# The first microseconds of a two-layer hybrid encoder put into one written order

## The chip, the cores and the metric

The kernel runs on one core of a Trainium2 chip. The metric is device time in microseconds of one execution. TensorE (PE) multiplies, VectorE (DVE) and ScalarE (ACT) do the elementwise work, GpSimd (POOL) fills constants and issues some DMAs, SyncE (SP) issues nearly all loads.

## The reference, cut to what matters

One sequence of 256 tokens with 1024 features goes through two layers. In each layer the tokens are normalised, four token mixers (A to D) take slices of one combined projection of the normalised tokens, the four results are gated and summed, and a feed-forward part follows. The edit touches the first normalisation and the first product behind it:

```
xf = x.astype(F32)
y = xf * lax.rsqrt(jnp.mean(xf * xf, axis=-1, keepdims=True) + EPS)
return (y * g.astype(F32)).astype(x.dtype)     # rmsnorm
...
h @ w_in          # slices 3 and 16 of it are the values of mixers A and D
```

## The kernel before, in words

All weights lie in units of 128 x 2048 numbers and are streamed from memory, each as two halves of 512 KB. Each f32 product is made of three fp32r matmuls (`mm3`): a half `raw` is cast on ACT to `hi`, and DVE subtracts to get the rest, `lo`; activations are held in the same way as `ahi` and `ali`. The three products are hi by hi, hi by rest and rest by hi. Four buffers hold `raw`, six `hi`, five `lo`.

The norm (class `Norm`) works on two tiles of 128 tokens, tt = 0 and 1. The squares of a token tile are summed in two halves: for the first half of tile 0 on ACT (`Square`), for its second on DVE (line 202), for tile 1 both on ACT. A square root on ACT, a reciprocal and two `SCALAR_TENSOR_TENSOR` on DVE (line 221) then scale the tile to `xni`; its gain `ng` comes from two matmuls with one row of ones. PE turns `xni` round, 128 x 128 at a time, against the matrix `ident`, into `nti` (line 234), which ACT and DVE split into `ahi` and `ali` (lines 235, 236).

The first product (`tok_units`) is units 3 and 16 together: for each token tile eight steps k, each three matmuls of 128 x 512 into `av`. Steps k = 0 to 3 use unit 3's two halves, k = 4 to 7 unit 16's. Tile 0 is done whole, then tile 1. After it come unit 5 (`bx`) and unit 6 (`bg`) of mixer B, units 0, 1, 2 and 4 (`aq`, `af`, `af`, `ag`) of mixer A, then unit 7 onwards (`c`) of mixer C; between them stand small products for filters, called `f` in the trace: line 369 and 372 make a hidden layer `hd`, a second sine chain on DVE called `sykb` ends in `h2s` (ACT), from which four more `f` products are made, and `bz` (gates of mixer B, with weights `bw`) whose results ACT turns by a sigmoid into `br` and `bi`. Sine, sigmoid, tanh and square root on ACT need tables that are loaded (`ACT_TABLE_LOAD`) where the kind changes.

The order of instructions on an engine is made when the program is built: a scheduler places instructions by priority on an estimated timeline. `tc.high_priority` raises a priority, and `behind(...)` keeps an instruction from standing ahead of a given one. `unit` issues a unit's loads on SP and its casts; all loads stand behind `x_in`, the load of the second token tile. `prepare`, `level_masks` and `filters` make constants on DVE and ACT; in layer 0 they stand behind the last weight load issued.

Of the kernel before, what the change touches and what calls it, by code (L numbers as in the profile page):

```python
# [41 lines left out]
NRAW, NHI, NLO = 4, 6, 5  # L42
@with_exitstack
def trunk(ctx: ExitStack, tc: tile.TileContext, A: dict, out: bass.AP, dbg=None):
    nc = tc.nc
    V, SC, G, PE = nc.vector, nc.scalar, nc.gpsimd, nc.tensor

    cp = ctx.enter_context(tc.tile_pool(name="cp", bufs=1))
    wp = ctx.enter_context(tc.tile_pool(name="wp", bufs=4))
# [38 lines left out]
    x = cp.tile([P, 2, D], F32, tag="x", name="x")  # L88
    nc.sync.dma_start(g0[:1], A["norm1_g"][0:1])
    nc.sync.dma_start(x[:, 0], A["x"][0:P])  # L90
    ident = const("ident", (P,))
    x_in = nc.sync.dma_start(x[:, 1], A["x"][P:S])
    with tc.issue_after(x_in.ins):
        par = const("par", (L, NPC), "params")

# [2 lines left out]
        return par[:, l, c : c + 1]  # L98


    last_load = [None]

    def behind(*ins):

        st = ExitStack()
        for i in ins:
            st.enter_context(tc.issue_after(i.ins))
        return st

    def unit(l, u, after=(), then=None, at=None):  # L110


        parts = []
        with tc.high_priority(offset=AHEAD):
            for hf in range(2):
                raw = wp.tile([P, 1024], F32, tag="raw", bufs=NRAW, name=f"raw{l}_{u}_{hf}")
                if at:
                    hi, lo = (get(f"{n}{l}_{u}_{hf}", F32R).rearrange("p a b -> p (a b)")
                              for n, get in zip(("hi", "lo"), at))
                else:  # L120
                    hi = wp.tile([P, 1024], F32R, tag="hi", bufs=NHI, name=f"hi{l}_{u}_{hf}")
                    lo = wp.tile([P, 1024], F32R, tag="lo", bufs=NLO, name=f"lo{l}_{u}_{hf}")
                with tc.issue_after(x_in.ins):
                    last_load[0] = nc.sync.dma_start(raw, A["wall"][l, u, :, hf * 1024 : hf * 1024 + 1024])
                with behind(*(then if hf and then else after)):
                    SC.copy(hi, raw)  # L126
                    V.tensor_tensor(lo, raw, hi.bitcast(F32), ALU.subtract)  # L127
                parts.append((hi, lo))
        return parts

    def root_table(last):

# [25 lines left out]
                        k + ft == 0, k + ft == 8)  # L158
        return ps

    def tok_units(ws, act, nms, at):

        rows = [t for w in ws for part in w for t in zip(*(p.rearrange("p (k c) -> k p c", k=2) for p in part))]
        out = []
        with ExitStack() as order:
            for tt in range(2):
                ps = big(nms[tt])
                out.append(ps)  # L170
                c = slice(tt * P, tt * P + P)
                for k, w in enumerate(rows):
                    if (tt, k) in at:
                        order.enter_context(behind(at[tt, k](out)))
                    mm = mm3(ps.rearrange("p a b -> p (a b)"),
                             [a[k // 2][:, k % 2, c] if type(a) is list else a[:, k, c] for a in act], w, k == 0, k == 7)
                order.enter_context(behind(mm))
        return out


    class Norm:


        def __init__(self, nm, gain, l=0):
            self.ss = wk.tile([P, 2, 3], F32, tag="ss", bufs=2, name=f"ss{nm}")
            self.rs = wk.tile([P, 2], F32, tag="rs", bufs=2, name=f"rs{nm}")
            if nm == "i":
                self.g = [mix(f"ng{c}").rearrange("p a b -> p (a b)") for c in range(2)]
                for c in range(2):
                    PE.matmul(self.g[c], ones[:1], g0[:1, c * 512 : c * 512 + 512], start=True, stop=True)  # L190
            else:
                g = w4(f"ng{nm}").rearrange("p a b -> p (a b)")
                src = A[gain]
                nc.gpsimd.dma_start(g, bass.AP(src.tensor, src.offset + l * D, [[0, P], [1, D]]))
                self.g = [g[:, c : c + 512] for c in (0, 512)]
            self.xn = [w4(f"xn{nm}{tt}").rearrange("p a b -> p (a b)") for tt in range(2)]
            self.nm, self.hi = nm, None

        def add(self, tt, i, c):

            if (self.nm, tt, i) == ("i", 0, 1):
                V.tensor_tensor_reduce(self.xn[tt][:, c], x[:, tt, c], x[:, tt, c], 1.0, 0.0, ALU.mult, ALU.add,
                                       self.ss[:, tt, 1:2])
            else:
                SC.activation(self.xn[tt][:, c], x[:, tt, c], AF.Square, accum_out=self.ss[:, tt, i : i + 1])
            if not i:
# [628 lines left out]

    SC.activation(epsb2, epsb, AF.Sqrt)
    nm = Norm("i", "norm1_g")
    for tt in range(2):
        for hf in range(2):
            nm.add(tt, hf, slice(hf * 512, hf * 512 + 512))  # L840
        if tt:
            nm.scale(1)
        else:
            nm.half(0)
            turned = nm.scaled, nm.last
    h = nm.out()

    def late(nm):

        return {(0, 6 + dd): lambda _, dd=dd: nm.turn(1, dd) for dd in range(2)}  # L850

    for l in range(L):
        pv = tok_units([unit(l, 3), unit(l, 16, *turned)], h, [f"av0{l}", f"av1{l}"], late(nm))
# [318 lines left out]
```

## Time and profile before

| | |
|---|---|
| median of 3 runs | 1001.65 us (1000.2 to 1003.1) |
| the profiled execution's own time | 999.49 us |
| its span in the trace | 997.6 us |
| PE busy | 976.9 us of the span |
| DVE, ACT busy | 655.4 us, 546.2 us |

The profiled execution is 1.9 us longer than its span, for what lies around the first and the last instruction. It is 2.2 us below the median of the unprofiled runs. Busy time of PE counts matmuls whose ends are modelled; at full clock two neighbouring 128x256 matmuls start 0.12 us apart, and two of 128x512 start 0.23 us apart.

### The profile page before, as it was taken

What the parts mean: (1) busy time and instruction counts of PE and PEld (TensorE: products, weight loads), DVE (VectorE), ACT (ScalarE), POOL (GpSimd) and SP (SyncE); (2) the same over time, 40 slices, a digit from 0 to 9 for tenths busy, and PEclk for the clock granted to TensorE, in tenths of its full rate; (3) what the DMA queues carried; (4) which work ended last, traced back from release to release, by engine and by line L of the source; (5) the groups of instructions that cost most, each with busy time, mean ns of one, the idle gap of its engine ahead of it and who ended that gap; (6) DMA issues with size and microseconds to landing.
All of it is one profiled execution on the core that took longest, in us unless ns stands there. A gap on an engine that the chain in (4) does not pass through costs nothing.

```text
span 997.6 us, 18829 instructions
## 1 busy us (share of the span) xinstructions
PE 976.9 (98%) x7770; PEld 913.2 (92%) x7770; DVE 655.4 (66%) x900; ACT 546.2 (55%) x815; POOL 48.1 (5%) x85
## 2 busy tenths in 40 slices
PE   7999999999999999999999999999999999999997
PEld 5889999999998999999989999999999889999996
DVE  6859894777766764455567679767667575555554
ACT  6696746545745544444457875554454464444442
POOL 0127200000000010000000000000000000000000
PEclk9999999999999999999999999999999999999999
DMA  8648455355555555555546445453465556555551
GB/s 286 202 133 217 135 170 171 116 170 159 183 174 164 187 169 190 188 186 180 186 148 210 162 158 160 158 177 106 163 228 173 170 161 211 187 182 189 187 172 43
DMA packets 51484, 172.41 MB, mean 173 GB/s; under 512 B 8716, under 2 KB 9413, under 8 KB 51398
## 3 DMA queue, kind: packets, MB, share of 16 engines
q1 hardware_dynamic: 47158, 163.41, 50.3%
q0 software_dynamic: 4240, 7.79, 3.1%
q8 instruction: 61, 1.00, 0.4%
q14 instruction: 25, 0.20, 0.1%
HBM read 170.08 MB, written 2.63 MB: 173 GB/s over the span
## 4 chain that ended last, share of the span: by engine, by line
PE 87%; DVE 5%; DMA 4%; ACT 2%; issue 1%; SPq 0%; DVEq 0%; ACTq 0%
PE f L142 9%; PE f L144 9%; PE f L143 8%; PE g L142 6%; PE g L144 6%; PE g L143 6%; PE acc L143 4%; PE acc L142 4%; PE acc L144 4%; DMA raw<-in_wall_dram 3%; DVE lo L127 2%; PE wo L143 1%; PE wo L144 1%; PE wo L142 1%; PE br L142 1%; PE br L143 1%
## 5 line engine op out<-in xcount | busy, mean ns | idle before, releaser
L127 DVE TENSOR_TENSOR lo<-raw,hi 128x1024 fp32r<-128x1024 f32 x304 | 370.2, 1222 | 223.0 <-PE f L143 109.5
L126 ACT CAST hi<-raw 128x1024 fp32r<-128x1024 f32 x304 | 317.5, 1051 | 294.3 <-PE f L144 99.8
L142 PE MATMUL f<-ahm,hi 128*128 128x256 f32 x640 | 181.1, 283 | 0.0
L144 PE MATMUL f<-alm,hi 128*128 128x256 f32 x640 | 181.1, 283 | 0.0
L143 PE MATMUL f<-ahm,lo 128*128 128x256 f32 x640 | 180.2, 282 | 0.0
L143 PEld LDWEIGHTS f<-ahm,lo 128*128 128x128 f32 x640 | 120.9, 189 | 1.0
L142 PEld LDWEIGHTS f<-ahm,hi 128*128 128x128 f32 x640 | 120.7, 189 | 0.9
L144 PEld LDWEIGHTS f<-alm,hi 128*128 128x128 f32 x640 | 120.4, 188 | 0.0
L142 PE MATMUL g<-ahi,hi 128*128 128x256 f32 x256 | 73.3, 286 | 2.1 <-ACT dvt L734 2.1
L144 PE MATMUL g<-alf,hi 128*128 128x256 f32 x256 | 72.8, 284 | 0.0
L142 PE MATMUL g<-ahf,hi 128*128 128x256 f32 x256 | 72.6, 283 | 0.2 <-ACT dvt L734 0.2
L143 PE MATMUL g<-ahf,lo 128*128 128x256 f32 x256 | 72.4, 283 | 0.0
L143 PE MATMUL g<-ahi,lo 128*128 128x256 f32 x256 | 72.3, 283 | 0.0
L144 PE MATMUL g<-ali,hi 128*128 128x256 f32 x256 | 72.3, 282 | 0.0
L143 PE MATMUL acc<-hi,fal 128*128 128x512 f32 x176 | 69.5, 395 | 0.0
L144 PE MATMUL acc<-lo,fah 128*128 128x512 f32 x176 | 69.3, 395 | 0.0
L142 PE MATMUL acc<-hi,fah 128*128 128x512 f32 x176 | 69.1, 395 | 0.0
L142 PEld LDWEIGHTS g<-ahi,hi 128*128 128x128 f32 x256 | 48.2, 188 | 3.3 <-ACT dvt L734 2.3
L142 PEld LDWEIGHTS g<-ahf,hi 128*128 128x128 f32 x256 | 48.2, 188 | 0.6 <-ACT dvt L734 0.4
L144 PEld LDWEIGHTS g<-alf,hi 128*128 128x128 f32 x256 | 48.2, 188 | 0.5 <-issue 0.3
L143 PEld LDWEIGHTS g<-ahi,lo 128*128 128x128 f32 x256 | 48.2, 188 | 0.2 <-issue 0.2
L143 PEld LDWEIGHTS g<-ahf,lo 128*128 128x128 f32 x256 | 48.2, 188 | 0.2 <-issue 0.2
(493 smaller groups left out, 2209.6 us busy)
## 6 DMA issues: line engine op xcount, KB each, us to landing
raw<-in_wall_dram SPq DMA_DIRECT2D x304, 512.0 KB, 4.6
bt<-bias POOLq DMA_DIRECT2D x8, 384.0 KB, 3.8
x<-in_x_dram SPq DMA_DIRECT2D x2, 512.0 KB, 6.1
bias<-tab POOLq DMA_DIRECT2D x16, 64.0 KB, 5.9
ngm<-in_norm_g_dram POOLq DMA_DIRECT2D x2, 512.0 KB, 4.3
out_dram<-x SPq DMA_DIRECT2D x4, 256.0 KB, 2.0
bias<-tab POOLq DMA_DIRECT2D x32, 16.0 KB, 4.3
ngf<-in_norm_g_dram POOLq DMA_DIRECT2D x1, 512.0 KB, 4.1
```

Of the source, the lines that this page charges most:

```text
L126: SC.copy(hi, raw)
L127: V.tensor_tensor(lo, raw, hi.bitcast(F32), ALU.subtract)
L142: PE.matmul(o, a[0], b[0], start=first, stop=False)
L143: PE.matmul(o, a[1], b[0], start=False, stop=False)
L144: return PE.matmul(o, a[0], b[1], start=False, stop=last)
```

## The change

The loads on SP are put in a new order: tokens 0, both halves of unit 3, tokens 1, both halves of unit 16. `ident` is no longer loaded (64 KB); POOL makes it with a memset and an `affine_select`. Eight 128 x 128 matmuls of ones by ones are put ahead of the gain's matmuls. The norm, the casts and the splits of the first two units (new function `first_unit`) are each placed behind the one written ahead of them. The product's steps go by turns: k = 0 to 5 for token tile 0, k = 0 to 5 for tile 1, then k = 6, 7 for tile 0 and for tile 1; the turning of tile 1 stands ahead of step 4 of tile 0 and step 0 of tile 1. The constants of `prepare` and what follows them are placed behind the last split of unit 16 also.

```
+    G.memset(ident, 0.0)
+    G.affine_select(out=ident, in_=ident, compare_op=ALU.not_equal, fill=1.0, base=0, pattern=[[-1, P]],
+                    channel_multiplier=1)
...
-    ident = const("ident", (P,))
-    x_in = nc.sync.dma_start(x[:, 1], A["x"][P:S])
+    raws = {}
+    for u, hf in ((3, 0), (3, 1), (16, 0), (16, 1)):
...
+        x_in = nc.sync.dma_start(raws[0, u, hf][0], A["wall"][0, u, :, hf * 1024 : hf * 1024 + 1024])
+        if (u, hf) == (3, 1):
+            nc.sync.dma_start(x[:, 1], A["x"][P:S])
...
+    def first_unit(u, hf):
+        raw, hi, lo = raws[0, u, hf]
+        return SC.copy(hi, raw), V.tensor_tensor(lo, raw, hi.bitcast(F32), ALU.subtract)
...
+                for _ in range(8):
+                    PE.matmul(self.g[0][:, 0:P], ones, ones, start=True, stop=True)
...
+        for hf in range(2):
+            then(*nm.add(0, hf, halves[hf]))
+        nm.scale(0)
+        then(*nm.scaled)
+        then(*first_unit(3, 0))
+        for dd in range(2):
+            nm.turn(0, dd)
+            then(*nm.last)
+        then(*nm.add(1, 0, halves[0]))
+        then(*first_unit(3, 1))
+        then(*nm.add(1, 1, halves[1]))
+        nm.scale(1)
+        then(*nm.scaled)
+        then(*first_unit(16, 0))
...
+            pv = tok_units(first, h, [f"av0{l}", f"av1{l}"], {(0, 4): lambda _: turn(0), (1, 0): lambda _: turn(1)},
+                           ((0, range(6)), (1, range(6)), (0, range(6, 8)), (1, range(6, 8))))
...
-            with behind(last_load[0]):
+            with behind(last_load[0], *begun):
```

What this does to the order, at three places. The first is DVE at the very start, from the statistics of token tile 0 on (`ssi` statistics, `xni_120` and `xni_121` the scaled tiles, `lo_3_0` the first half's rest). Before:

```order
L202 ISA xni_93,ssi<-x 128x512
L202 ISA ssi 128x1
L208 TENSOR_SCALAR ssi<-ssi 128x1
L213 RECIPROCAL rsi<-rsi 128x1
L221 SCALAR_TENSOR_TENSOR xni_93<-x,rsi,ng_89 128x512
L221 SCALAR_TENSOR_TENSOR xni_93<-x,rsi,ng_90 128x512
L208 TENSOR_SCALAR ssi<-ssi 128x1
L213 RECIPROCAL rsi<-rsi 128x1
L221 SCALAR_TENSOR_TENSOR xni_94<-x,rsi,ng_89 128x512
L221 SCALAR_TENSOR_TENSOR xni_94<-x,rsi,ng_90 128x512
L127 TENSOR_TENSOR lo_3_0_127<-raw_3_0_125,hi_3_0_126 128x1024
L236 TENSOR_TENSOR ali<-nti_104,ahi 128x4x128
```

With the change:

```order
L228 TENSOR_SCALAR ssi<-ssi 128x1
L222 ISA xni_120,ssi<-x 128x512
L222 ISA ssi 128x1
L234 RECIPROCAL rsi<-rsi 128x1
L242 SCALAR_TENSOR_TENSOR xni_120<-x,rsi,ng_108 128x512
L242 SCALAR_TENSOR_TENSOR xni_120<-x,rsi,ng_109 128x512
L144 TENSOR_TENSOR lo_3_0_88<-raw_3_0_86,hi_3_0_87 128x1024
L257 TENSOR_TENSOR ali<-nti_133,ahi 128x4x128
L257 TENSOR_TENSOR ali<-nti_140,ahi 128x4x128
L228 TENSOR_SCALAR ssi<-ssi 128x1
L144 TENSOR_TENSOR lo_3_1_92<-raw_3_1_90,hi_3_1_91 128x1024
L234 RECIPROCAL rsi<-rsi 128x1
```

The small `TENSOR_SCALAR` on `ssi` now stands ahead of the reduce, the first half's rest ahead of the first `ali`, and the scaling of tile 1 behind two rests; by the diff the rest of unit 16's first half comes right behind that scaling.

The second place is ACT between the last query product `aq` and the first gate of mixer B (`br`). Before:

```order
L137 CAST bwh_510<-bw_506 128x512
L454 ACT_TABLE_LOAD
L454 ACTIVATE bt_500<-bt_500 128x512
L346 ACT_TABLE_LOAD
L346 ACTIVATE sykb_308<-sykb_308 128x256
L137 CAST h2s_316<-sykb_308 128x256
L126 CAST hi_4_1_849<-raw_4_1_848 128x1024
L137 CAST bwh_518<-bw_514 128x512
L515 COPY kqe_633<-aq_649 128x512
L516 COPY kqo_634<-aq_649 128x512
```

With the change, from the sine's table load on (the sigmoids of the first `af`, `sf_773` and `sk_774`, stand just ahead):

```order
L367 ACT_TABLE_LOAD
L367 ACTIVATE sykb_319<-sykb_319 128x256
L549 ACTIVATE kqe_644<-sk_774,omlb 128x256 x2
L136 CAST hi_8_0_1004<-raw_8_0_1003 128x1024
L152 CAST h2s_327<-sykb_319 128x256
L136 CAST hi_8_1_1010<-raw_8_1_1009 128x1024
L544 ACT_TABLE_LOAD
L544 ACTIVATE sf_844<-af_794 128x512
L545 ACTIVATE sk_845<-af_794 128x512
L548 ACTIVATE sf_844<-sf_844,lb,omlb 128x256 x2
L549 ACTIVATE kqo_645<-sk_845,omlb 128x256 x2
L496 ACTIVATE br_537<-bz_539,par 128x256
```

The sine of `sykb` and `h2s` stood ahead of the copies of `aq`; now they stand behind the sigmoids of the first `af`, with a table load on either side, and the first `br` stands behind the second `af` as well.

The third place is PE where the first `h2s` products stand. Before, the first of them behind 23 matmuls of the first `af` unit (`af_712`):

```order
L144 MATMUL af_712<-ali,hi_1_0_701 128x256
L142 MATMUL af_712<-ahi,hi_1_0_701 128x256
L143 MATMUL af_712<-ahi,lo_1_0_702 128x256
L142 MATMUL f_000_323<-h2s_316,w3s_291 128x256
L143 MATMUL f_000_323<-h2s_316,w3s_291 128x256
L142 MATMUL f_010_324<-h2s_316,w3s_291 128x256
L143 MATMUL f_010_324<-h2s_316,w3s_291 128x256
```

With the change, behind both `af` units and 22 matmuls of `ag`:

```order
L158 MATMUL ag_865<-ahi,lo_4_0_855 128x256
L159 MATMUL ag_865<-ali,hi_4_0_854 128x256
L157 MATMUL ag_865<-ahi,hi_4_0_854 128x256
L157 MATMUL f_000_334<-h2s_327,w3s_302 128x256
L158 MATMUL f_000_334<-h2s_327,w3s_302 128x256
L157 MATMUL f_010_335<-h2s_327,w3s_302 128x256
L158 MATMUL f_010_335<-h2s_327,w3s_302 128x256
```

They stand 95 matmuls of 128x256 further back; the first `bz` moves with them and stands right behind the eighth.

## Rows read from the trace of the kernel before

**Rows 1.** The profile page, part 1: busy time, share of the span and instructions of each engine.

```profile
PE 976.9 (98%) x7770; PEld 913.2 (92%) x7770; DVE 655.4 (66%) x900; ACT 546.2 (55%) x815; POOL 48.1 (5%) x85
```

**Rows 2.** The waits of PE over the whole run: who waited, for which engine's tile and line; us in total, times, longest.

```profile
PE f L142 <- ACT h2s L137: 3.3, 2, 2.1
PE nti L234 <- DVE xni L221: 2.7, 2, 1.4
PE ng L190 <- DMA g<-in_norm_g_dram: 2.5, 1, 2.5
PE g L142 <- ACT dvt L734: 2.3, 2, 2.1
```

**Rows 3.** Busy time by stretch of the span: the stretch and its length, then busy us of PE, PEld (weight loads), DVE, ACT and POOL with instructions in brackets, granted clock, DMA share, GB/s.

```profile
0.00:18.00 18.00, 12.87 (x35) 8.37 (x36) 10.77 (x22) 12.31 (x23) 0.44 (x6) 1.00 0.87 286
...
50.00:75.00 25.00, 23.63 (x192) 21.32 (x193) 14.97 (x25) 23.85 (x55) 5.42 (x9) 1.00 0.48 133
...
104.00:152.00 48.00, 45.92 (x556) 44.09 (x555) 46.75 (x72) 27.70 (x42) 2.16 (x4) 1.00 0.49 153
```

**Rows 4.** SP's DMA issues at the start, in order of time: start, us, queue, line, what.

```profile
2.49 2.20 SPq L124 DMA_DIRECT2D raw<-in_wall_dram  x4
...
8.13 0.33 SPq L865 DMA_DIRECT2D idft<-in_dft_dram  x1
9.60 0.33 SPq L296 DMA_DIRECT2D maskf<-in_masks_dram  x1
...
13.53 0.31 SPq L359 DMA_DIRECT2D zd<-in_zT_dram  x1
```

**Rows 5.** The timeline of the first 14 us, all engines: start, us, engine, line, operation, out<-in, count [idle time before <- what ended it].

```profile
2.47 3.75 PE L190 MATMUL ng<-g,ones 1*128 1x512 f32 x4 [2.47 <-DMA g<-in_norm_g_dram]
...
5.24 0.69 DVE L202 CUSTOM_DVE_ANT_0 xni<-x 128x512 f32<-128x512 f32 x1 [4.36 <-DMA x<-in_x_dram]
...
6.80 1.41 DVE L221 SCALAR_TENSOR_TENSOR xni<-x,rsi,ng 128x512 f32<-128x512 f32 x2
...
7.60 1.97 PE L234 MATMUL nti<-ident,xni 128*128 128x128 f32 x8 [1.39 <-DVE xni L221]
...
9.71 1.03 ACT L126 CAST hi<-raw 128x1024 fp32r<-128x1024 f32 x1
...
11.36 1.22 DVE L127 TENSOR_TENSOR lo<-raw,hi 128x1024 fp32r<-128x1024 f32 x1
...
11.61 0.78 PE L142 MATMUL av<-hi,ahi 128*128 128x512 f32 x1
...
12.49 1.28 DVE L236 TENSOR_TENSOR ali<-nti,ahi 128x512 fp32r<-128x512 f32 x2
...
13.23 0.79 PE L143 MATMUL av<-hi,ali 128*128 128x512 f32 x1
```

**Rows 6.** The timeline of PE, 14 to 27 us, two pairs of neighbours and the first matmul of the next unit (columns as above).

```profile
14.25 0.63 PE L142 MATMUL av<-hi,ahi 128*128 128x512 f32 x1
14.68 0.63 PE L143 MATMUL av<-hi,ali 128*128 128x512 f32 x1
...
26.29 0.39 PE L144 MATMUL av<-lo,ahi 128*128 128x512 f32 x1
26.52 0.28 PE L142 MATMUL bx<-ahi,hi 128*128 128x256 f32 x1
```

**Rows 7.** The timeline of PE, 30 to 64 us: the rows that had to wait, and the first `bz`.

```profile
34.89 0.70 PE L372 MATMUL f<-hd,hw 64*128 64x256 f32 x2 [0.78 <-ACT hd L346]
...
46.51 0.36 PE L142 MATMUL af<-ahi,hi 128*128 128x256 f32 x1 [0.99 <-DVE bxc L441]
...
50.76 0.39 PE L142 MATMUL f<-h2s,w3s 64*128 64x256 f32 x2 [1.28 <-ACT h2s L137]
...
54.08 0.39 PE L142 MATMUL bz<-bxsh,bwh 128*128 128x256 f32 x1
```

**Rows 8.** The timeline of ACT, 48 to 72 us.

```profile
48.56 1.28 ACT L346 ACT_TABLE_LOAD   x1
49.85 0.42 ACT L346 ACTIVATE sykb<-sykb 128x256 f32<-128x256 f32 x1
50.30 0.40 ACT L137 CAST h2s<-sykb 128x256 fp32r<-128x256 f32 x1
...
59.52 0.47 ACT L475 ACTIVATE br<-bz,par 128x256 f32<-128x256 f32 x1
...
71.04 1.08 ACT L527 ACTIVATE sf<-sf,lb,omlb 128x256 f32<-128x256 f32 x2
```

**Rows 9.** The timelines of ACT and of DVE, 78 to 106 us: three rows by which the lead is followed.

```profile
78.99 0.56 ACT L434 ACTIVATE cu<-c,par 128x256 f32<-128x256 f32 x1 [0.48 <-PE c L144]
...
83.64 0.47 DVE L405 SCALAR_TENSOR_TENSOR hpm<-hf,fnn 128x256 f32<-128x256 f32 x1
...
105.11 1.23 DVE L493 SCALAR_TENSOR_TENSOR br<-bE,br 128x1024 f32<-128x1024 f32 x1 [2.01 <-ACT bs L488]
```

**Rows 10.** The timeline of PE around 150 us.

```profile
150.72 0.38 PE L142 MATMUL g<-ahi,hi 128*128 128x256 f32 x1 [2.08 <-ACT dvt L734]
150.94 0.29 PE L143 MATMUL g<-ahi,lo 128*128 128x256 f32 x1
151.06 0.28 PE L144 MATMUL g<-ali,hi 128*128 128x256 f32 x1
```

More of the change, by code (lines that the diff above doesn't have):

```diff
@@ L80, in trunk @@
     G.memset(ones, 1.0)
+    ident = cp.tile([P, P], F32, tag="ident", name="ident")
+    G.memset(ident, 0.0)
+    G.affine_select(out=ident, in_=ident, compare_op=ALU.not_equal, fill=1.0, base=0, pattern=[[-1, P]],
+                    channel_multiplier=1)
     g0 = w4("g0").rearrange("p a b -> p (a b)")
@@ L90, in trunk @@
     nc.sync.dma_start(x[:, 0], A["x"][0:P])
-    ident = const("ident", (P,))
-    x_in = nc.sync.dma_start(x[:, 1], A["x"][P:S])
+    raws = {}
+    for u, hf in ((3, 0), (3, 1), (16, 0), (16, 1)):
+        raws[0, u, hf] = [wp.tile([P, 1024], F32 if n == "raw" else F32R, tag=n, bufs=b, name=f"{n}0_{u}_{hf}")
+                          for n, b in (("raw", NRAW), ("hi", NHI), ("lo", NLO))]
+        x_in = nc.sync.dma_start(raws[0, u, hf][0], A["wall"][0, u, :, hf * 1024 : hf * 1024 + 1024])
+        if (u, hf) == (3, 1):
+            nc.sync.dma_start(x[:, 1], A["x"][P:S])
     with tc.issue_after(x_in.ins):
@@ L98, in pcol @@
         return par[:, l, c : c + 1]
-    last_load = [None]
+    last_load = [x_in]
     def behind(*ins):
@@ L159, in feat_unit, with tok_units @@
         return ps
-    def tok_units(ws, act, nms, at):
+    def tok_units(ws, act, nms, at, turns=((0, range(8)), (1, range(8)))):
         rows = [t for w in ws for part in w for t in zip(*(p.rearrange("p (k c) -> k p c", k=2) for p in part))]
@@ L167, in tok_units @@
         with ExitStack() as order:
-            for tt in range(2):
-                ps = big(nms[tt])
-                out.append(ps)
+            for tt, ks in turns:
+                if len(out) == tt:
+                    out.append(big(nms[tt]))
+                ps = out[tt]
                 c = slice(tt * P, tt * P + P)
-                for k, w in enumerate(rows):
+                for k in ks:
                     if (tt, k) in at:
@@ L175, in tok_units @@
                     mm = mm3(ps.rearrange("p a b -> p (a b)"),
-                             [a[k // 2][:, k % 2, c] if type(a) is list else a[:, k, c] for a in act], w, k == 0, k == 7)
+                             [a[k // 2][:, k % 2, c] if type(a) is list else a[:, k, c] for a in act], rows[k],
+                             k == 0, k == 7)
                 order.enter_context(behind(mm))
@@ L837, in trunk, with then @@
     nm = Norm("i", "norm1_g")
-    for tt in range(2):
+    with tc.high_priority(), ExitStack() as order:
+        def then(*ins):
+            order.enter_context(behind(*ins))
+        halves = [slice(hf * 512, hf * 512 + 512) for hf in range(2)]
         for hf in range(2):
[L840 to L845, printed above, removed]
+            then(*nm.add(0, hf, halves[hf]))
[11 more added lines that the diff above has]
+        then(*first_unit(16, 0))
     h = nm.out()
@@ L852, in trunk, with turn @@
     for l in range(L):
-        pv = tok_units([unit(l, 3), unit(l, 16, *turned)], h, [f"av0{l}", f"av1{l}"], late(nm))
+        if l:
+            pv = tok_units([unit(l, 3), unit(l, 16, *turned)], h, [f"av0{l}", f"av1{l}"], late(nm))
+        else:
+            begun = []
+            def turn(dd):
+                pe = nm.turn(1, dd)
+                if dd:
+                    with tc.high_priority(), behind(*nm.last):
+                        begun.extend(first_unit(16, 1))
+                return pe
+            first = [[raws[0, u, hf][1:] for hf in range(2)] for u in (3, 16)]
+            pv = tok_units(first, h, [f"av0{l}", f"av1{l}"], {(0, 4): lambda _: turn(0), (1, 0): lambda _: turn(1)},
+                           ((0, range(6)), (1, range(6)), (0, range(6, 8)), (1, range(6, 8))))
         va, v0 = u2(f"av{l}"), u2(f"dv0{l}")
```

7 lines of the change are left out of this document (4 added, 3 removed).

## The prediction

> **What bounds the kernel now.** I read the page's busy times first: PE is busy 976.9 of 997.6 us [rows 1], so a gain can only come from the 20.7 us in which it is not, or from matmuls that run at half clock. The list of PE's waits says where the first kind lies [rows 2]: 2.5 us for the norm's gain, 2.7 us for `xni` before the turns, 3.3 us for `h2s` (2.1 of them in layer 1), 2.3 us for `dvt`; the rest are small. The stretches then show who is full where [rows 3]: of the first 18 us PE is busy 12.87; from 50 to 75 us ACT is the full one (23.85 of 25), from 104 to 152 us DVE (46.75 of 48), with PE at 45.92. So a lead that PE wins at the start must pass two stretches in which another engine is almost full. The two orders are alike again from about the 1660th matmul on, near 260 us; all that the change can move lies ahead of that, and what lead is left there is the gain.
>
> The start in detail [rows 5]: tile 0 is scaled from 6.80, turned from 7.60, unit 3's first half cast from 9.71, its rest made from 11.36, and the product becomes dense only at 13.23, when `ali` (12.49, 1.28 for two) is there. It starts at half clock: neighbours stand 0.43 us apart at 14.25, and 0.23 apart at 26.29 [rows 6], which is the step from 1.2 to 2.4 GHz. After the last `av` matmul `bx` starts at 26.52.
>
> **Loads.** With SP's queue full, each further issue starts as a landing frees a place: 8.13 (tokens 1), 9.60 (unit 3, first half), then 13.53 for unit 16's second half, three halves later, so 1.31 us each [rows 4]. Without ident's 64 KB (an eighth of a half, about 0.2 us) and with unit 3 ahead of tokens 1, unit 3 lands at about 7.9 and 9.4, tokens 1 at 10.7, unit 16 at 11.95 and 13.3.
>
> **The first product.** Tile 0's reduce (0.69) now stands behind the small DVE instruction that waits for ACT's sum. That costs about 0.5 us: scaling from 7.3, turns from 8.1 to 10.1. The cast of unit 3's first half runs inside that time (7.9 to 9.0) instead of at 9.71, its rest (1.22) to 10.2. The first `av` can start at 10.1 instead of 11.61, the second, which needs `ali`, at 10.85 instead of 13.23. So the product starts over 2 us earlier, but it doesn't keep that. Tokens 1 land 2.6 us later, two squares (0.7 each by the reduce's row, with unit 3's second cast, 1.03, between), root and reciprocal bring the scaling of tile 1 to 13.75 to 15.1, and only behind it DVE makes unit 16's first rest, to 16.3. The twelve matmuls of k = 0 to 3 end by 14.6 to 16.0. So PE goes on at 16.3 with six matmuls (0.23 to 0.43 each) and a turn, to 17.7 to 18.35. Thirty `av` at 0.23 and one `f` at 0.43 follow: `bx` at 25.1 to 25.75 against 26.52. **Gain 0.8 to 1.4 us, I take 1.1.** The eight matmuls of ones wait for nothing but POOL's memset and run from 1.05 to about 4.5 (0.43 each, the nearest row's pitch), the gain's until 6.4 to 8.0, about when the scaling needs them; POOL makes `ident` in the 8 us before the turns. If they cost anything it is up to 0.7 us at the scaling, which the wait until 16.3 swallows.
>
> The gain's one-row matmuls keep PE busy for 3.75 us from 2.47, and yet the eight turns at 7.60 take 1.97, 0.25 each, and the product starts at a 0.43 pitch [rows 5, 6]: that work did not raise the clock. The Trainium skill ("TensorE: Matmul & The Clock Gate", Part 1) says that the clock starts throttled, is released by sustained activity of the array and falls again when it idles. By it, ones over all 128 rows may release the clock where one row did not, and `bx` would stand at the lower end, 25.1; by the row alone they would not, and it is 25.75. No run here shows ones over all rows yet. The sum goes by the middle.
>
> **Four waits that move.** All times are after-times from counted orders and these rows' durations (128x256 matmuls 0.12 apart).
> - `hd`: PE idled 0.78 before 34.89 [rows 7]. Now 45 more matmuls (5.4 us) stand ahead of that `f`, so PE is there at about 38.3; the sine stands behind two more casts and a `bxc` and ends at about 38.5. Gain 0.65, between 0.3 and 0.8.
> - `af`: PE idled 0.99 before 46.51 [rows 7], for the last taps of `bxc`. Now it waits for `bgl`, made at about 43.95, and is there at 25.4 + 144 x 0.12 + 0.7 = 43.4. Gain 0.5, between 0 and 1.0.
> - `h2s`: PE idled 1.28 before 50.76 [rows 7]. The first product of `h2s` moves behind 95 more matmuls, to 43.95 + 118 x 0.12 = 58.1; ACT, which loads a table before the sine (1.28, 0.42, cast 0.40 [rows 8]) and now does it behind the first `af`'s sigmoids, has `h2s` at 56 to 58. Gain 1.3.
> - `bz`: the second row of `bz` needs the first `br` read out by ACT. Before, that stood at 59.52 behind one table load. Now ACT does, behind `h2s`, a cast (1.03), a table load (1.28), two sigmoids of the second `af` (0.5 each), two `sf` (1.08), two `kqo` (as long) and then `br` (0.47): 6 us, so 62 to 64. PE is there at 58.1 + 3.3 = 61.4, since the like row of `f` and `bz` took it from 50.76 to 54.08 [rows 7]. Loss 1.4 more than the 0.6 of before, between 0 and 2.5.
>
> Sum: -1.1 - 0.65 - 0.5 - 1.3 + 1.4 = **-2.2 us** on PE at about 75 us. ACT's first `cu` moves from 78.99 to about 76.8 and DVE's last `hpm` from 83.64 to about 80.5 [rows 9], since DVE carries fewer constants there: DVE, which sets 104 to 152, gets a lead of about 3. In that stretch the work is the same; `br` waited 2.0 us for ACT's `bs` at 105.11 [rows 9], so not all of it need pass. The `dvt` wait (2.08 at 150.72 [rows 10]) has one cast more ahead of it on ACT (1.05) and a rest less on DVE (1.22): no net change. I take 2.7, between PE's 2.2 and DVE's 3.2. The profiled execution becomes 999.49 - 2.7 = 996.8; the median shown is 2.16 above that execution, so 1001.65 - 2.7 = 998.95.
>
> Covers: the constants of `prepare` and the splits of the transform matrices now run after unit 16; the weight loads behind them move 2 to 2.5 us later, and the cover is the lead that loads have on their use: no wait of PE names a load but the gain's at the start [rows 2]. Without that cover they would cost PE up to those 2.5 us once. The bias tables' small products move 10 us back; POOL's DMAs that hang on them were nearly done by 104 (2.16 us of POOL in the stretch behind it [rows 3]), and mixer D reads them only past 150. Neither is priced.
>
> **Rivals.**
> - *The lead is given back* (0.2): only the 1.1 of the start stays, because ACT, full from 50 to 75 us, has two more table loads (2.56 us) there and `bz` takes 2.5 instead of 1.4, or DVE's full stretch swallows it. 1001.65 - 1.0 = 1000.6. For it: rows 3. Against: DVE's own lead.
> - *A larger gain* (0.15): every term at its good end: `h2s` at 56, so that `bz` waits for nothing at all (its 0.6 goes too): -1.4 - 0.8 - 1.0 - 1.3 - 0.6 = -5.1, so 996.5. For it: `h2s` may well be done 2 us ahead of PE. Against: five terms must all fall well, and DVE pass them on.
> - *Slower, by the clock* (0.08): the product now stops and starts until 16.3. If the clock is at 1.2 GHz when the last 30 `av` start, and stays there through them, they take 0.2 us more each, +6; with the -2.7 that is +3.3, about 1005. It decides if the pitch behind 17.7 is 0.43. Against: after the 2.08 us wait at 150.72 the next neighbours still stand 0.12 apart [rows 10].
> - *Slower, by ACT* (0.07): `br` comes 3 us after its need and `c` behind it passes that on to DVE's full stretch, with the tables 2.56 late: +1.5 to +3, about 1004.
>
> The forecast has 0.5. About 0.3% (3 us, so 998.65) is what a measurement of this kernel can tell from no change. A little less than half of the forecast's own chance lies beyond it (0.23), and the larger gain: faster 0.38. The two last rivals make slower, less a part that stays within 3 us: 0.13. The rest, 0.49, is no change that can be told. The range runs from the larger gain's far side, 995.5, to 1002.5, which leaves the slower cases out, and little else.
>
> **What would show it.** After: the ones before 5 us; `av` from about 10.1, a gap before 16.3 that ends with unit 16's rest; `bx` at 25.1 to 25.75; the idle rows for `hd` and `af` below 0.6, none for the first `h2s`, a new one of about 2 for `br`; `cu` at 76.8; the `dvt` row some 2.7 ahead of 150.72. The forecast is wrong if the `av` pitch is 0.43 beyond 18 us, if `bx` is not ahead of 26, or if ACT reaches the first `br` only after 65.

## The result: slower, and the profile after

The changed kernel takes 1004.46 us (median of nine, 1002.63 to 1007.28), the kernel before 999.99 beside it: a ratio of 1.0052, interval 1.0039 to 1.0065. It is slower by 3.9 to 6.5 us, where I forecast 2.7 faster. The execution in the profile took 1006.34, its span 1004.5. The page's busy times after (beside [rows 1]):

```profile
PE 982.4 (98%) x7786; PEld 919.1 (91%) x7786; DVE 654.4 (65%) x900; ACT 546.4 (54%) x815; POOL 48.6 (5%) x87
```

DVE and ACT do the same work as before. PE has the 16 instructions of the eight products of ones more and is busy 5.5 us longer. These ones take 3.78 of it; the rest is matmuls over the same weights that ran slower. The list of PE's waits after (beside [rows 2]):

```profile
PE g L157 <- ACT dvt L755: 4.5, 2, 4.3
PE f L157 <- ACT h2s L152: 3.5, 1, 3.5
PE bz L157 <- ACT br L496: 1.6, 1, 1.6
...
PE ng L208 <- POOL ones L80: 1.0, 1, 1.0
PE af L157 <- DVE bgl L476: 0.8, 1, 0.8
PE nti L255 <- DVE xni L242: 0.7, 1, 0.7
```

The start does what it should: `ng` and `nti` wait 1.7 us together, 5.2 before. But the wait for `dvt`, which I left at 2.1, is 4.3. The start on PE, in its timeline (beside [rows 5, 6]):

```profile
1.03 3.78 PE L208 MATMUL ng<-ones 128*128 128x128 f32 x16 [1.03 <-POOL ones L80]
...
7.68 1.32 PE L255 MATMUL nti<-ident,xni 128*128 128x128 f32 x8 [0.72 <-DVE xni L242]
8.99 0.80 PE L157 MATMUL av<-hi,ahi 128*128 128x512 f32 x1
...
14.28 0.63 PE L158 MATMUL av<-hi,ali 128*128 128x512 f32 x1
14.71 0.63 PE L159 MATMUL av<-lo,ahi 128*128 128x512 f32 x1
...
25.34 0.28 PE L157 MATMUL bx<-ahi,hi 128*128 128x256 f32 x1
```

`bx` starts at 25.34 for 26.52. Where the same matmuls lie behind both, PE is 2.1 to 2.6 us ahead in its weight products from 82 us up to the last `dv` at 145 (2.28 at rows of `dk` and `dv`; forecast: 2.2). Only the weight products have this lead: the recurrence's own products `s`, whose input DVE makes, start between 0.7 later and 1.8 earlier than before. So the loss shows from 145 us on, where PE has no weight product left and waits first for DVE's `ab` and then for `dvt`. Its timeline there after (beside [rows 10]; before, the `s` like the first row starts at 147.63 with no wait):

```profile
146.55 0.69 PE L570 MATMUL s<-ab 64*64 64x64 f32 x32 [1.01 <-DVE ab L591]
151.56 0.58 PE L157 MATMUL g<-ahi,hi 128*128 128x256 f32 x1 [4.32 <-ACT dvt L755]
151.94 0.41 PE L158 MATMUL g<-ahi,lo 128*128 128x256 f32 x1
152.29 2.08 PE L601 MATMUL s<-ab 64*128 64x128 f32 x16
...
155.99 0.28 PE L157 MATMUL g<-ahi,hi 128*128 128x256 f32 x1
156.11 0.28 PE L158 MATMUL g<-ahi,lo 128*128 128x256 f32 x1
```

The first `g` starts at 151.56 for 150.72: the lead is gone, and 0.84 more. Then the sixteen `s` take 2.08 us, where the kernel before needs 1.16 (at 153.31), and neighbours are not 0.12 apart until about 156. The same 38 matmuls (twenty `g`, sixteen `s`, two `ao`), from the first `g` on, take 5.74 us after and 3.93 before. So PE is 2.65 behind when they are done: 0.84 by the waits and 1.81 by slower matmuls. The stretches (columns as in [rows 3]: PE, PEld, DVE, ACT, POOL, granted clock) say why; first the changed kernel:

```profile
104.00:152.00 48.00, 42.67 (x529) 40.88 (x528) 46.40 (x72) 26.65 (x39) 8.73 (x15) 0.96 0.56 160
148.00:150.00 2.00, 0.00 (x0) 0.00 (x0) 2.00 (x4) 1.95 (x5) 0.00 (x0) 0.66 0.13 47
150.00:152.00 2.00, 0.44 (x2) 0.44 (x2) 0.61 (x2) 1.97 (x5) 0.00 (x0) 0.50 0.65 209
152.00:154.00 2.00, 2.00 (x18) 1.77 (x17) 0.00 (x0) 0.00 (x0) 0.00 (x0) 0.50 0.13 53
154.00:156.00 2.00, 2.00 (x14) 1.77 (x13) 0.00 (x0) 1.08 (x2) 0.00 (x0) 0.64 0.00 0
```

and the kernel before:

```profile
150.00:152.00 2.00, 1.28 (x10) 1.28 (x11) 1.86 (x3) 1.96 (x4) 0.00 (x0) 1.00 0.69 236
152.00:154.00 2.00, 2.00 (x24) 1.87 (x24) 0.00 (x0) 0.23 (x1) 0.00 (x0) 1.00 0.67 225
```

During the 4.3 us wait the granted clock falls from 1.00 to 0.50, which is 1.2 GHz, and stays there until about 155. The Trainium skill ("TensorE: Matmul & The Clock Gate", Part 1) says that the clock is throttled again when the array idles; the trace agrees.

Why the wait is longer, though PE came earlier, is on ACT and DVE. ACT after:

```profile
146.79 1.65 ACT L610 COPY P<-Pc 64x256 f32<-64x256 f32 x4 [3.79 <-DVE Pc L605]
148.47 1.04 ACT L136 CAST hi<-raw 128x1024 fp32r<-128x1024 f32 x1
149.42 1.50 ACT L611 COPY P<-s 64x256 f32<-64x256 f32 x4
150.93 1.07 ACT L755 COPY dvt<-dv 128x512 f32<-128x512 f32 x2
```

and before:

```profile
146.91 1.65 ACT L589 COPY P<-Pc 64x256 f32<-64x256 f32 x4 [0.80 <-DVE Pc L584]
148.57 1.50 ACT L590 COPY P<-s 64x256 f32<-64x256 f32 x4
150.08 0.59 ACT L734 COPY dvt<-dv 128x512 f32<-128x512 f32 x1
```

The copies `P<-Pc` start when DVE's last masked copy into `Pc` is made: 146.79 and 146.91, the same time in both, so they now wait 3.79 us for it, not 0.80. DVE has no idle time there in either kernel (110 to 150 us, before and then after):

```profile
110.00:150.00 40.00, 38.64 (x467) 37.34 (x459) 40.00 (x63) 19.76 (x29) 0.00 (x0) 1.00 0.50 160
```

```profile
110.00:150.00 40.00, 36.23 (x453) 35.04 (x443) 40.00 (x64) 18.71 (x27) 3.03 (x5) 0.98 0.55 162
```

and `br`, with which I let that stretch begin, starts at 105.26 for 105.11 [rows 9]:

```profile
102.92 0.69 DVE L153 TENSOR_TENSOR fhl<-ft,fhh 128x512 fp32r<-128x512 f32 x1 [2.48 <-ACT fhh L152]
103.52 1.22 DVE L137 TENSOR_TENSOR lo<-raw,hi 128x1024 fp32r<-128x1024 f32 x1
104.66 0.69 DVE L153 TENSOR_TENSOR dql<-dq,dqh 128x512 fp32r<-128x512 f32 x1
105.26 1.22 DVE L514 SCALAR_TENSOR_TENSOR br<-bE,br 128x1024 f32<-128x1024 f32 x1
```

Before, DVE waited 2.01 there for ACT's `bs`. Now it waits 2.48 a little earlier for another result of ACT, `fhh`, and then does one rest and `dql` ahead of `br`; `bs`, which starts at 103.83 for 104.02, is not what holds it any more. The rest that is done early is made up for by another: between `br` and the last `Pc` stand twelve rests in both kernels, and it is 41.4 us from one to the other after and 41.7 before. On top, a cast (1.04) now stands between the copies into `P`, so `dvt` comes at 150.93 for 150.08. ACT came no earlier with `bs` and `fhh` because, 1.5 us ahead at `cu` (77.48), it then stood for weights:

```profile
88.01 1.05 ACT L136 CAST hi<-raw 128x1024 fp32r<-128x1024 f32 x1 [3.79 <-DMA raw<-in_wall_dram]
...
92.51 1.05 ACT L136 CAST hi<-raw 128x1024 fp32r<-128x1024 f32 x1 [1.58 <-DMA raw<-in_wall_dram]
```

The first of these waits comes from a late issue. SP puts a load into a `raw` buffer when DVE's rest has freed it. Of the five loads from 76 to 94 us the first is issued at 78.31 before, when the rest of 77.07 is made, and at 82.73 after, because DVE has put the `hpm` ahead and makes that rest at 81.48. SP had waited up to 7.6 us for such a rest, and up to 5.2 before. The five loads, by the view of `raw` from 76 to 94 us, before:

```profile
L124 SPq DMA_DIRECT2D raw<-in_wall_dram x5: 328/328/328, 78.3 to 89.4; - x5
...
DMA to landing us min/median/max: 5.8/5.8/5.8
```

and after:

```profile
L134 SPq DMA_DIRECT2D raw<-in_wall_dram x5: 327/328/328, 82.7 to 92.8; - x5
...
DMA to landing us min/median/max: 5.2/8.2/8.3
```

The first landed in 5.2 us, sooner than any before. For the second wait the load took 8.2 for 5.8. POOL's queue has 20 of the bias tables' small DMAs in these 18 us, but 23 before, too. So it is not shown that they make these loads slower.

### The profile page after: what moved, and what is told of

The parts are those of the page before. It is cut to its first block, busy times and chain, and to the rows that moved or that the text cites. A ratio compares the mean times of both kernels' runs of the same rounds, so it can differ in the third digit from the quotient of the medians.

```text
span 1004.5 us, 18874 instructions
## 1 busy us (share of the span) xinstructions
PE 982.4 (98%) x7786; PEld 919.1 (91%) x7786; DVE 654.4 (65%) x900; ACT 546.4 (54%) x815; POOL 48.6 (5%) x87
## 4 chain that ended last, share of the span: by engine, by line
PE 87%; DVE 5%; DMA 3%; ACT 3%; issue 1%; DVEq 0%; SPq 0%; ACTq 0%
PE f L157 9%; PE f L159 8%; PE f L158 8%; PE g L157 6%; PE g L158 6%; PE g L159 6%; PE acc L158 4%; PE acc L159 4%; PE acc L157 4%; DMA raw<-in_wall_dram 3%; DVE lo L137 2%; PE wo L159 1%; PE wo L158 1%; PE wo L157 1%; PE br L157 1%; PE br L158 1%
## 5 line engine op out<-in xcount | busy, mean ns | idle before, releaser
L137 DVE TENSOR_TENSOR lo<-raw,hi 128x1024 fp32r<-128x1024 f32 x300 | 365.5, 1222 | 228.5 <-PE f L158 112.7
L136 ACT CAST hi<-raw 128x1024 fp32r<-128x1024 f32 x300 | 313.5, 1051 | 301.8 <-PE f L159 102.6
L159 PEld LDWEIGHTS g<-ali,hi 128*128 128x128 f32 x256 | 48.5, 189 | 0.2 <-issue 0.2
```

The costliest lines, as they stand in the source:

```text
L159: return PE.matmul(o, a[0], b[1], start=False, stop=last)
```

## The experiments

My theory after this reading: DVE's full stretch fixes when `dvt` comes, so PE's lead becomes waiting, and the longer wait costs clock. Rivals: the loads held up by the bias tables are the cause; the new beginning itself costs; or DVE's stretch only shows a loss made elsewhere. Ratios are to the kernel before.

**The loads: e1 and e4.** POOL's spreading of the bias tables waits for a late tile: `filt` in the changed kernel (e1), the filters' norm at about 77 us in the kernel before (e4).

```
+        def spread(F):
+            scr = cp.tile([P, 1], F32, tag="scr", name="scr")
+            with behind(G.tensor_copy(scr[:1], F[:1, 0, 1, 0, 0:1])):
...
+            bias = spread(F)
```

> The changed kernel, with the DMAs that write the bias tables held on POOL until the first filter matrix is there (near 95 us); the scheduler then also puts two casts behind the Relu bs on ACT. Theory A (the start's 1.2 us and the 2.3 us lead are real, but the bias DMAs, moved by 10 us, push weight loads out of the way at 80 to 92 us, so that ACT's bs at 104 us gains nothing, PE then runs out of work and idles over 4 us, and its clock falls): ACT's waits for weights between 84 and 93 us (5.4 us together) shrink below 2 us, bs comes at or before 102 us, PE's wait for dvt is 2.5 us or less at full clock, time 998 to 1000 us. Rival B (the recurrence is bound by its own length and nothing ahead of it moves it): bs and the dvt wait stay within 0.5 us, time 1003 to 1006.

> The kernel before, with only the bias-table DMAs held on POOL until 77 us, about where the changed kernel has them; order of all other engines as before. Theory A: weight loads between 80 and 92 us take over 7 us from issue to landing instead of 5.8, ACT waits for a weight there by 1 us or more, bs moves from 104.0 to 104.5 or later, time 1 to 3 us above before. Rival (the bias DMAs don't matter, ACT's order does): landings and bs within 0.3 us, time as before within 0.5 us.

e1: 1002.71, ratio 1.0031 (1.0015 to 1.0047). e4: 999.96, 1.0004 (0.9988 to 1.0020). In e1 the loads land in 4.8 us and `bs` starts at 102.30, 1.5 earlier, and `br` at 103.39, 1.87 earlier. But the scheduler put one more rest into DVE's stretch, thirteen for twelve: the last `Pc` is made only 0.46 earlier, and PE waits 4.32 as before, with the clock at 0.50. My theory had 998 to 1000 us and missed; the rival's 1003 is missed by a little. By the ratios this edit takes about 2 us of the 5 away, though the intervals overlap; its profile shows that DVE's earlier start alone does not shorten the wait. In e4 the loads land in 4.6 us, not over 7, and the time is as before: tables as late as the changed kernel's cost the old beginning nothing, as its rival said.

**The ones: e3.** The changed kernel without them.

```
-                for _ in range(8):
-                    PE.matmul(self.g[0][:, 0:P], ones, ones, start=True, stop=True)
```

> The changed kernel without the eight matmuls of ones; every other instruction stands where it stood. Theory A: the turns take 2 us instead of 1.3 and bx starts within 0.5 us of 25.34; time 1004 to 1005. Rival (the early burst of full-array work is what makes the clock fall again at 9 us and later): av at full clock from before 14 us, bx below 24.5, time below 1002.5.

1003.33, 1.0038 (1.0024 to 1.0052): most of the penalty stays, so that much is not theirs. The interval overlaps the changed kernel's; whether the ones cost a part of it can't be told. `bx` starts at 25.33, as with them.

**The clock: e2, e8, e7.** Eight products of ones into the wait, in the changed kernel (e2), in the kernel before (e8), and in e1 (e7).

```
                     s128 = [mix(f"s{l}{lev}{q}").rearrange("p a (b c) -> p a b c", b=2) for q in range(2)]
+                    if l == 0:
+                        with tc.high_priority():
+                            for _ in range(8):
+                                PE.matmul(s128[0][:, 0, 0], ones, ones, start=True, stop=True)
```

> The changed kernel, with eight matmuls of ones into a PSUM tile that is overwritten later, put on PE inside its long wait near 147 us. Theory A: the wait itself stays, but the clock is still at full speed behind it: the sixteen s matmuls near 152 us take under 1.2 us instead of 2.1, and the time falls by 1.5 to 3 us, to 1001.5 to 1003. Rival (the clock is a by-product and hides behind other waits): granted clock 1.00 there, time within 0.5 us of 1004.5.

> The kernel before with eight matmuls of ones inside its own wait near 148 us (2.3 us long). Theory A: that wait is short enough that the clock rarely falls in it, so the fill changes it by less than 1 us: 998.5 to 1000. Rival (the filling is a gain for any kernel, by 3 us): 996 to 997.

> The changed kernel with both edits: bias DMAs held on POOL until near 95 us, and eight matmuls of ones inside PE's long wait near 147 us. Theory A: the two add up, bs near 102.3 as with the held DMAs alone and the clock at 1.00 from 150 to 155 us as with the filled wait alone: 999 to 1001. Rival (the fill's gain was the order of g and s behind it, which the hold undoes): above 1002.

e2: 1001.44, 1.0019 (1.0003 to 1.0035), 3 us less than the changed kernel. e8: 999.88, 1.0012 (0.9996 to 1.0028), nothing. e7: 1000.98, 1.0014 (0.9998 to 1.0031), nothing beyond e2. PE in e2:

```profile
146.71 2.05 PE L600 MATMUL s<-ones 128*128 128x128 f32 x16
...
150.57 1.16 PE L605 MATMUL s<-ab 64*128 64x128 f32 x16 [1.19 <-DVE ab L591]
```

The sixteen `s` take 1.16, as before, and the clock is 1.00 in 150 to 160. The edit also moved them ahead of the first `g`, so the 3 us are not purely the clock's. In the profile some 2.9 of them lie between the 1200th and the 1500th matmul (about 145 to 180 us), which take 38.2 us in the changed kernel, 35.3 in e2 and 32.3 in the kernel before.

**DVE's stretch, with work left out: e5 and e6.** For units 13, 14, 15, 17 and 18 of layer 0 the rest is 0 x raw, which takes DVE less time.

```
+                    if l == 0 and u in (13, 14, 15, 17, 18):
+                        V.tensor_scalar(lo, raw, 0.0, None, ALU.mult)
```

> The changed kernel with half of DVE's work on ten weight halves of its full stretch left out (units 13, 14, 15, 17, 18: lo is 0 times raw, one source, instead of raw minus hi), some 6 us less on DVE between 107 and 150 us. Theory A2 (the lead of 2.3 us that PE has at 145 us is worth nothing because DVE is full there and ends at the same time with or without it): the copies behind the recurrence come 4 us or more earlier, PE waits for dvt less than 1.5 us, its clock stays up, and this kernel is 1 to 3 us faster than the kernel before with the same work left out. Rival (the change loses by its order alone, DVE or not): it is still 3 us or more slower than that one.

> The kernel before with the same work left out on DVE (units 13, 14, 15, 17, 18: lo is 0 times raw). Theory A2: its wait for dvt goes as well, time 997 to 998.5, that is 1 to 3 us above the changed kernel with the same work left out. Rival: 3 us or more below that one.

e5 (changed): 996.29, 0.9970 (0.9957 to 0.9984). e6 (before): 996.59, 0.9973 (0.9960 to 0.9986). The last `Pc` comes at 140.8 and 139.6, no wait is left at 147, the clock is 1.00: the penalty is gone. But the changed kernel is no faster than the other either, where my theory had 1 to 3 us and the rival the opposite. The profiled pair can't say why: in e5's profiled execution, the slowest of its ten, the clock fell to 0.59 behind the wait for `bz`, and the lead was gone before DVE's stretch (0.4 ahead to 0.2 behind from 92 to 145 us). It is 2.2 ahead at 300 us because e6's clock falls behind a wait for `h2s` of 1.95, and loses 3.2 at 745, in a wait of layer 1 with a lower clock behind it. So this pair doesn't test whether the lead passes, and why the two come out equal stays open.

**DVE's stretch, with work moved to POOL: e9 and e10.** The subtraction for four halves on POOL.

```
-                    V.tensor_tensor(lo, raw, hi.bitcast(F32), ALU.subtract)
+                    (G if (l, u, hf) in ((0, 14, 1), (0, 15, 1), (0, 17, 1), (0, 18, 1)) else V).tensor_tensor(
+                        lo, raw, hi.bitcast(F32), ALU.subtract)
```

> The changed kernel with four of the subtractions of DVE's full stretch (second halves of units 14, 15, 17 and 18) done on POOL, which is idle there; nothing left out. Theory A2: DVE's stretch is up to 4.9 us shorter, the copies behind the recurrence come 3 us or more earlier if POOL's work doesn't slow DVE's, PE's long wait goes below 2 us and its clock stays up: 996 to 998.5, faster than both kernels. Rival (POOL and DVE slow one another): DVE's own rows of the stretch lengthen by as much as they lose, time 1000 or more.

> The kernel before with the same four subtractions on POOL. Theory A2: its wait of 2.1 us for dvt goes, 997 to 998.5, and the changed kernel with the same edit is 0 to 2.3 us faster than this one. Rival: POOL and DVE slow one another, 999 or more.

1003.84, 1.0043 (1.0026 to 1.0059), and 1005.90, 1.0062 (1.0046 to 1.0079): a failed tool. POOL's and DVE's timeline in e9:

```profile
118.27 2.37 POOL L137 TENSOR_TENSOR lo<-raw,hi 128x1024 fp32r<-128x1024 f32 x1 [2.22 <-PE dk L159]
```

```profile
118.32 2.87 DVE L591 TENSOR_TENSOR ab<-W,kqe 128x512 f32<-128x512 f32 x1
```

An `ab` that takes 0.69 elsewhere takes 2.87 beside POOL's subtraction: DVE is held while POOL works, and what was moved came back as waiting. It tells nothing on the theory.

**ACT's place of `dvt`: e11 and e15.** The copies into `dvt` ranked high (e11), and that with e2's edit (e15).

```
-            SC.copy(vt[:, :, :, g - 1], ps.rearrange("p c (m r) -> p c r m", r=4))
+            with tc.high_priority():
+                SC.copy(vt[:, :, :, g - 1], ps.rearrange("p c (m r) -> p c r m", r=4))
```

> The changed kernel with the copies dvt at high priority on ACT, so that they stand ahead of three of the four copies P from s. Theory A2: dvt at 150.2 or before instead of 150.9, PE's wait 0.7 us shorter, the clock still falls: 1003 to 1004. Rival (order on ACT alone makes the wait): the wait falls by 2 us or more and the time below 1002.

> The changed kernel with the copies into dvt ranked high on ACT and the eight products of ones in the wait near 147. Theory: the wait of 3.1 stays but the clock stays at 1.00 behind it, so it is 1 to 3 us below the run with dvt ahead alone: 998 to 1000. Rival (the clock did not cost there): 1000 to 1001.5, as dvt ahead alone.

e11: 1000.46, 1.0004 (0.9992 to 1.0017); in the profile, of the slowest of its ten executions, the wait is 3.1 and the clock 0.75 in 150 to 155. One line of order takes 4 us of the 5 away. My theory had 1003 to 1004 and was wrong on the time: the wait shrank by only 1.26, and the kernel gained what the rival forecast. e15: 1000.58, 1.0001 (0.9988 to 1.0014). My theory missed there: the clock stays at 1.00, but nothing is won, and the sixteen `s`, ahead of `g` again, wait 1.19 us for DVE's `ab`. So e2's 3 us and e11's 4 don't add up; either takes away the same loss: the 300 matmuls named above take 35.5 us in e11, 35.3 in e2.

**DVE's stretch, by order alone: e12, e13, e14, e16.** The casts and rests of units 24 and 25 in layer 0 are written down behind the last masked copy into `Pc`, in the changed kernel (e12) and in the kernel before (e13). e14 and e16 are the same two with e11's edit.

```
+                late = last_pc if l == 0 and u in (24, 25) else ()
-                with behind(*(then if hf and then else after)):
+                with behind(*(then if hf and then else after), *late):
                     SC.copy(hi, raw)
                     V.tensor_tensor(lo, raw, hi.bitcast(F32), ALU.subtract)
...
+                        if lev == 5 and l == 0:
+                            last_pc[:] = [pred]      # pred: the copy_predicated into Pc
```

> The changed kernel, with the casts and rests of units 24 and 25 in layer 0 written down behind the last masked copy into Pc. On DVE the two rests of unit 24 then stand behind that copy and not ahead of it, so 2.4 us of the full stretch leave the way to it; on ACT a cast of unit 25 stands ahead of P<-Pc and not behind it. Nothing is left out. Theory (DVE's full stretch and the cast on ACT make the wait at 147-151, and the wait lets the clock fall): last Pc near 144.3, first copy into dvt near 148, TensorE's wait ahead of the first g 1.0 to 2.4 us for 4.3, the granted clock in 150-155 back above 0.9, time 997.5 to 1000.5. Rival (the loss belongs to the new beginning or to its loads, and DVE's stretch only shows it): above 1002, the time comes back as another wait before 300 us.

> The kernel before with the same edit: the control. dv ends at 148.2 here, so only its 2.1 us wait ahead of the first g can go, and no clock is won back. Theory: 997.5 to 999.5 against 1000.0, so the edit is worth some 4 us more to the changed kernel than to the kernel before. Rival: the edit is worth the same to both, 997 to 999 here and 1002 in the changed kernel.

> The changed kernel with units 24 and 25 behind the last Pc and the copies into dvt ranked high on ACT, where they then stand inside the copies P<-s. Theory: first copy into dvt near 147, wait ahead of the first g under 1.5 us, the clock at 1.00; 997 to 999.5, and faster than the kernel before if the lead of 2.3 is kept. Rival (something later takes the lead back however early g starts): 999.5 to 1001.5.

> The kernel before with both edits of e14 (units 24 and 25 behind the last Pc, copies into dvt ranked high on ACT): the control for e14, which took 998.32 at a ratio of 0.9984 to the kernel before. dv ends at 148.2 here, so at most the 2.1 us wait ahead of the first g can go. Theory (the new beginning is worth its lead once the wait is gone): 999 to 1000, so e14 stays 0.7 to 1.7 us below it. Rival (e14 is faster by its two edits alone, and the new beginning adds nothing): 998 to 998.7, as e14.

| | beginning | median us | ratio (interval) |
|---|---|---|---|
| e12 | changed | 1000.39 | 1.0007 (0.9994 to 1.0021) |
| e13 | before | 999.59 | 0.9996 (0.9984 to 1.0007) |
| e14 | changed | 998.32 | 0.9984 (0.9970 to 0.9998) |
| e16 | before | 997.61 | 0.9978 (0.9966 to 0.9989) |

The first `g` in e12, e13, e14 and e16, each from its own timeline:

```profile
149.69 0.39 PE L160 MATMUL g<-ahi,hi 128*128 128x256 f32 x1 [3.18 <-ACT dvt L760]
```

```profile
150.52 0.38 PE L145 MATMUL g<-ahi,hi 128*128 128x256 f32 x1 [2.15 <-ACT dvt L739]
```

```profile
147.89 0.57 PE L160 MATMUL g<-ahi,hi 128*128 128x256 f32 x1 [1.94 <-ACT dvt L761]
```

```profile
149.12 0.39 PE L145 MATMUL g<-ahi,hi 128*128 128x256 f32 x1 [0.91 <-ACT dvt L740]
```

e12 takes 4 us off the changed kernel, e13 (just outside its range) nothing that can be told off the old one: most of the penalty hangs on the order at 140 to 151 us. The last `Pc` in e12 comes at 145.4, not 144.3, and the wait is still 3.2, longer than I expected; the clock stays up for the first 1.4 us behind it and is then half until about 155 (0.66 in 150 to 155). But its first `g` starts 1.0 ahead of the kernel before [rows 10] and not 0.8 behind.

e14 and e16 tell what the lead is worth. Both beat both kernels of this case, and by the ratios, whose intervals overlap, the rival of e16 was right: the two edits make the gain, and the new beginning adds nothing that can be told. e14 is in its range by time, but its wait (1.94, not under 1.5) and its clock are not as I expected. The last `dv` row starts at 145.67 in e14 and at 147.93 in e16, so 2.26 of lead are there. At the first `g` 1.23 are left, since PE waits 1.94 for 0.91. Then the stretch 148 to 152, in e14 and in e16:

```profile
148.00:152.00 4.00, 4.00 (x22) 4.00 (x22) 2.20 (x3) 2.59 (x5) 0.00 (x0) 0.58 0.83 280
```

```profile
148.00:152.00 4.00, 3.09 (x26) 2.88 (x26) 3.43 (x4) 3.78 (x8) 0.00 (x0) 1.00 0.63 196
```

The clock is 0.58 for 1.00, and neighbours stand 0.21 apart until 151.25. The sixteen `s` start at 153.04 for 152.29 in e16, but in e14 four more `g` (0.5 us) stand ahead of them. At equal work e14 is 0.2 to 0.3 *behind*: in this pair the lead is spent in two parts, 1.0 in the wait and 1.5 in the clock behind it.

A further 0.9 us goes at full clock and without a wait. The last two groups of `sc`, products of mixer D, stand one behind the other in e14,

```profile
174.58 0.44 PE L790 MATMUL sc<-dk,dq 64*64 64x64 f32 x6
174.95 0.38 PE L785 MATMUL sc<-dkh,dqh 64*128 64x256 f32 x1
```

and are mixed, two by two, in e16:

```profile
175.30 0.39 PE L764 MATMUL sc<-dkh,dqh 64*128 64x256 f32 x2
...
175.85 0.46 PE L769 MATMUL sc<-dk,dq 64*64 64x64 f32 x16
```

The same 42 steps take 3.25 us in e14 and 2.36 in e16, so e14 is 1.2 behind at 178 us, and 1.1 at the end. The changed kernel has e14's order, the kernel before e16's. No run changes this alone.

## Why the prediction was wrong, step by step

- **The start: in its range, in part by luck.** `bx` stands at 25.34, inside 25.1 to 25.75. The first `av` stood at 8.99 for my 10.1, unit 16's first rest at 14.60 for 16.3; the pitch of 0.43 gave it back. The upper end was added up wrongly: six `av` at 0.43 make 2.6 us, so 26.2. Over the eleven profiled executions with the new beginning `bx` stands between 24.86 and 25.93, over the seven with the old one between 25.89 and 27.80. The ones brought the clock up early in some executions only, and it didn't last. In five of the ten profiled executions with ones (this one, e2, e12, e14, e15) the gain's four matmuls behind them take 1.98 to 2.22 us, which is full clock; in the other five they take 3.78, and in all eight without ones 3.75. Then PE waited 0.7 to 2.2 us for `xni`, the granted clock fell (here 0.92 in 7 to 9 us, 0.50 in 9 to 11), and `av` began at half clock in all five. Only here were the turns much faster for it (1.32; 1.74 to 2.03 in the others, 1.97 before). Without ones (e3) `bx` is at 25.33 too. The Trainium skill ("TensorE: Matmul & The Clock Gate", Part 1), by which sustained activity releases the clock, had put them at the lower end; the trace agrees for the gain's matmuls of those five executions, and not for `av`.
- **`hd`, `af`, `h2s`, `bz`: right.** The waits for `hd` and the first `h2s` are gone, `af` waits 0.8 for my 0.5 left over, the new `bz` wait is 1.65 for about 2. PE's 2.2 became about 2.3. `cu` starts at 77.48 for 76.8, the last `hpm` starts at 81.09 for about 80.5.
- **The step that failed: "I take 2.7, between PE's 2.2 and DVE's 3.2".** I had read that DVE is full from 104 to 152, and let the lead run through it on the ground that DVE got a lead of its own. DVE's lead ended at `br`: 105.26 for 105.11, because ACT came no earlier. The 2.01 wait there [rows 9] should have told me that DVE's start is ACT's to give. So the lead was worth 0, not 2.7: the last `Pc` came at the same time, PE's wait grew from 2.08 to 4.32, and the clock, at 0.50 behind it, cost 1.81 more. The rival "the lead is given back" named this place, but let the 1.1 of the start stay and gave the longer wait no price.
- **"No net change" at `dvt`: wrong.** I set a cast of 1.05 on ACT off against a rest of 1.22 on DVE. From `br` on the work to the last `Pc` shrank by 0.3 only, the cast counted almost in full: `dvt` 0.85 later. e11 and e12, which move what stands ahead of `dvt`, get some 4 us back.
- **The clock rival: right mechanism, wrong place.** I looked for it at the start and argued from the full clock after a 2.08 us wait [rows 10]. That row says nothing of a wait of 4.3, into which an unpassed lead of 2.3 makes it. At equal work that cost 1.81 here. Its "about 1005" lies near the result by luck: it was added up from thirty slow `av` at the start, and those ran at 0.23.
- **"Neither is priced": the cover was thin.** I had the loads 2 to 2.5 us later, and covered. The one that ACT stood 3.79 us for was issued 4.4 later, and ACT stood 5.4 for two. What that costs is not shown by itself: e1, in which the loads land in 4.8 us, is some 2 us faster, and DVE's stretch takes back most of what `br` gains there.
- **The rest.** Of the 6.9 us by which the two spans differ, 2.65 are lost by 157 us and some 0.9 by the order of the `sc` (3.49 behind at 187 us). PE is 3.38 behind at 226 us, and 6.10 at 300 us, behind the one wait for `h2s` (3.5, before 2.1 [rows 2]): 1.5 by the wait, the rest by the clock behind it (0.57 in 261 to 265 us). In e1 that wait is 0.7 and in e3 1.9, with the same beginning; I take it for a difference between executions, as the profiled one, 1006.34, is 1.9 above its median. That is argued, not shown. Open too is why e5 and e6 come out equal.

## What to carry to other kernels

A lead passes a stretch in which another engine is full only if that engine has less to do in it, or starts it earlier and puts nothing else ahead of the instruction that is waited for (e1 did, and gained 0.46 of 1.87 us); follow its first instruction to what releases it, and its last to who waits. A lead that doesn't pass is not merely lost: it lengthens TensorE's next wait, and the clock can fall in it. Before giving work a new beginning, clear what stands ahead of the releasing instruction at the end of the full stretch: two edits of order there won 2.2 us by the ratio (e16), the whole new beginning none that can be told.

## What the runs showed of the hardware that I had not expected

- **Short waits and the clock.** Behind waits of 2.08 us (before) and 2.15 (e13) matmuls ran at full clock; behind 2.05 (e4) and 1.94 (e14) the granted clock fell (0.66 in 150 to 155 us; 0.58 in 148 to 152). So it did behind the wait of 1.67 for `bz` in e5 (0.59 in 64 to 66), and not behind the like one of 1.65 in the changed kernel. All waits over 3 us at the first `g` (after, e1, e3, e11, e12) had a lower clock at their end or soon behind it. So a wait near 2 us may or may not cost.
- **A clock brought up early was lost again before the product.** After ones the gain's matmuls ran at full clock in five of ten executions, and `av` started at half clock all the same. It reaches the 0.23 pitch at 11.2 to 16 us with ones and at 12.7 without (e3), so one pair of executions tells nothing here. In the kernel before the granted clock reads 1.00 for the first 18 us [rows 3] while `av` neighbours stand 0.43 apart [rows 6]: at the start the pitch is the surer sign.
- **POOL holds DVE up** in two-input work: an `ab` took 2.87 and another 2.26 for 0.69 in e9, while POOL's like subtraction took between 2.4 and 5.1 us in e9 and e10. The Trainium skill ("GPSIMD Engine Reference", 1. Specifications) says that GpSimd's memory interfaces are shared with VectorE, with contention for instructions with two inputs; the trace agrees.
